# Placing a pair's sums and one cast of x later on VectorE, at the seam between a hand-planned schedule and a steady loop

## The chip, the cores and the metric

The kernel runs on one core of one Trainium2 chip. The metric is device time in microseconds; a profiled execution also has a span, from its first to its last instruction. Ratios are the mean time of one kernel's runs over the mean of the other kernel's runs of the same rounds, so not quite the ratio of the medians that are quoted beside them.

## The reference

```python
x: (16, 512, 1024) float32;  w1, w2: (1024, 768) float32
y1 = np.matmul(x, w1)
y2 = np.matmul(x, w2)
return np.tanh(y1) * y2
```

Every variant below gave correct outputs.

## The kernel before

The 8192 rows of x are 64 tiles of 128 rows. The first six are done plainly. The rest go in 29 pairs, and each pair makes two **units**, an even one for w1 (which ends in tanh) and an odd one for w2 (which ends in the multiply and the store). A unit uses a Strassen-type scheme: seven products p1 to p7 of 128 x 512 blocks of x with blocks of w, in place of eight. For that, a pair needs four sums of blocks of x on VectorE:

```python
def s_block(i, n, eng):
    s = spool.tile([P, KH, P], f16, tag=n, name=n)
    a, b, op = {"s1": ("a21", "a22", ALU.add), "s2": ("s1", "a11", ALU.subtract),
                "s3": ("a11", "a21", ALU.subtract), "s4": ("a12", "s2", ALU.subtract)}[n]
    pin((nc.vector if eng == "dve" else nc.gpsimd).tensor_tensor(s, st[i, a], st[i, b], op))
    st[i, n] = s

PRODUCTS = {"p1": ("a11", "b11"), "p2": ("a12", "b21"), "p3": ("s4", "b22"), "p4": ("a22", "t4"),
            "p5": ("s1", "t1"), "p6": ("s2", "t2"), "p7": ("s3", "t3")}
```

The blocks a11 to a22 come out of a DMA transpose of x in fp16, and VectorE makes the fp16 copy (the cast). After the products, VectorE adds two parts out of PSUM; one of the additions, c22, reads the bank that p4 then goes on accumulating into:

```python
# name: (engine, cost, due in slots, needs, ...)   [cut: the other operations of a unit]
"p2": ("pe", 0.65, -2, ["seed"], unit_product, (u, "p2", "a", False, True)),
"p3": ("pe", 0.65, 2, ["s5"], unit_product, (u, "p3", "d", False, True)),
"c12": ("dve", 0.55, 3, ["p3", "u2"], add_out, (u, "d", "u2", "c12")),
"p7": ("pe", 0.65, 3, ["u2"], unit_product, (u, "p7", "b", False, False)),
"c22": ("dve", 0.55, 4, ["p7", "s5"], add_out, (u, "b", "s5", "c22")),
"p4": ("pe", 0.65, 6, ["c22"], unit_product, (u, "p4", "b", False, True)),
```

Up to unit 9 the order on each engine is written out by hand (the planned part). From unit 10 on, each operation gets a time in slots of 0.65 us, the time from one product's start to the next in the trace (93.09 to 93.74 in the prediction's timeline), and the sorted times are the program order on every engine. Unit u begins at slot 7u. In the trace VectorE kept to that order where data were ready sooner: c22, ready at about 94.60 us (the prediction's estimate), ran at 96.09, behind s2. This is the code that the change touches:

```python
for i in range(FIRST, PAIRS):          # FIRST = 6
    z = 14 * i - 6
    at(slot(z - 7), blocks, i)
    for j, n in enumerate(("s1", "s2", "s3", "s4")):
        at(slot(z - 5.5 + 1.3 * j), s_block, i, n, "dve")
    at(slot(z - 1.4), out_scales, i)
    if i == FIRST:
        continue
    for h in range(2):
        if i > FIRST + 1:
            at(slot(z - 46 + 4 * h), load_x, HEAD + 2 * i + h)
        at(slot(z - 30 + 4 * h), abs_x, i, h)
    late = 1.1 * (i == FIRST + 1)
    at(slot(z - 25 + late), scale_x, i)
    for h in range(2):
        at(slot(z - 24 + late + 4 * h), cast_x, i, h, "dve")
        at(slot(z - 24 + late + 4 * h), transpose_x, i, h)
```

## Time and profile before

| | before |
|---|---|
| time, median of the first 3 runs | 317.22 us (316.65 to 317.24) |
| span of the profiled execution | 315.3 us |
| TensorE busy | 307.9 us (98%) |
| VectorE busy | 244.8 us (78%) |
| ScalarE busy | 230.5 us (73%) |

With TensorE busy for 307.9 of 315.3 us, a change of order on VectorE can help only where TensorE waits. The prediction shows the lines that say where. In timeline lines the columns are start, duration, engine, line, operation, output and inputs, shape and count; a bracket at the end tells how long the engine had been idle and what ended it.

### The profile page before, as it was taken

To read this page: it belongs to the slowest core of one execution; us is meant where nothing else is said; L and a number is where in the kernel's file an instruction comes from. 1 tells how busy PE (TensorE), PEld (TensorE's weight loads), DVE (VectorE), ACT (ScalarE), POOL (GpSimd) and SP (SyncE) were. 2 spreads that over 40 slices of the span, in tenths; PEclk is the share of its full clock that TensorE was granted. 3 is DMA by queue.
4 is the path that set the end of the run, shared out by engine and by line. 5 is a ranking of instruction groups with operands and counts; after the bars stand their busy time and mean duration, and the time that the engine had idled before them with its cause. 6 is when DMAs were issued, how large, how long until landed. Compare 5 with 4: busy or idle time off the path is not lost.

```text
span 315.3 us, 5481 instructions
## 1 busy us (share of the span) xinstructions
PE 307.9 (98%) x1890; PEld 185.5 (59%) x1895; DVE 244.8 (78%) x571; ACT 230.5 (73%) x453; POOL 4.3 (1%) x10
## 2 busy tenths in 40 slices
PE   8999999999998999999999999999999999999994
PEld 5756656666555555555555556555555555555652
DVE  2688978888887778877777897777789777777743
ACT  3788789786887777778777777877777778876551
POOL 0000000000000000000000000000000000000003
PEclk9999999999999999999999999999999999999998
DMA  7999498999999998999999989999998899996222
GB/s 289 406 400 369 95 311 245 262 263 264 308 318 267 287 278 258 246 231 287 268 255 242 285 239 224 299 252 283 242 251 265 263 246 282 234 238 168 101 101 102
DMA packets 82300, 80.59 MB, mean 256 GB/s; under 512 B 63584, under 2 KB 64096, under 8 KB 82272
## 3 DMA queue, kind: packets, MB, share of 16 engines
q1 hardware_dynamic: 81408, 78.27, 89.0%
q10 hardware_dynamic: 864, 1.97, 1.6%
q8 instruction: 15, 0.25, 0.3%
q14 instruction: 13, 0.11, 0.1%
HBM read 39.85 MB, written 25.17 MB: 206 GB/s over the span
## 4 chain that ended last, share of the span: by engine, by line
PE 86%; DMA 6%; DVE 3%; ACT 2%; issue 1%; DVEq 0%; SPq 0%; ACTq 0%
PE bank L401 79%; PE bank L267 4%; DMA x_f<-in_x_dram 3%; DMA xT<-x_h 3%; PE bank L270 2%; PE bank L223 1%; ACT junk L340 1%; DVE x_h L360 1%; DVE o L287 1%; DVE t L318 1%; ACT b L313 0%; DVE c L423 0%; DVE o L437 0%; ACT x_h L362 0%; DVE t L322 0%
## 5 line engine op out<-in xcount | busy, mean ns | idle before, releaser
L401 PE MATMUL bank<-t,s 128*128 128x384 f16 x696 | 131.6, 326 | 0.4 <-DVE t L318 0.4
L401 PEld LDWEIGHTS <-s 128*128 128x128 f16 x928 | 90.6, 98 | 61.1 <-issue 0.8
L401 PEld LDWEIGHTS <-xT 128*128 128x128 f16 x696 | 67.9, 98 | 48.0 <-issue 2.2
L401 PE MATMUL bank<-b,xT 128*128 128x384 f16 x464 | 93.8, 326 | 0.2 <-ACT b L313 0.2
L423 DVE TENSOR_TENSOR c<-bank,u 128x384 f32<-128x384 f32 x58 | 32.0, 554 | 43.6 <-PE bank L401 41.1
L340 ACT ACTIVATE junk<-x_f 128x1024 bf16<-128x1024 f32 x58 | 60.8, 1049 | 2.6 <-DMA x_f<-in_x_dram 2.5
L431 ACT ACTIVATE th<-c,out_r 128x384 f32<-128x384 f32 x58 | 35.3, 609 | 21.9 <-DVE c L423 21.9
L401 PE MATMUL bank<-t,xT 128*128 128x384 f16 x232 | 47.0, 326 | 0.8 <-DVE c L423 0.8
L401 PE MATMUL bank<-b,s 128*128 128x384 f16 x232 | 47.1, 327 | 0.0
L418 ACT ACTIVATE u<-bank 128x384 f32<-128x384 f32 x58 | 28.2, 487 | 19.7 <-PE bank L401 19.3
L360 DVE TENSOR_SCALAR x_h<-x_f,pr 128x1024 f16<-128x1024 f32 x55 | 41.0, 747 | 0.2
L414 ACT ACTIVATE bank<-bank 128x384 f32<-128x384 f32 x58 | 27.8, 481 | 12.7 <-DVE o L437 10.1
L423 DVE TENSOR_TENSOR c<-bank,s 128x384 f32<-128x384 f32 x58 | 32.2, 555 | 6.0 <-PE bank L401 5.0
L431 ACT ACTIVATE th<-bank,out_r 128x384 f32<-128x384 f32 x58 | 33.3, 573 | 4.5 <-PE bank L401 4.5
L437 DVE SCALAR_TENSOR_TENSOR o<-bank,out_r,th 128x384 f32<-128x384 f32 x58 | 35.4, 611 | 0.9 <-PE bank L401 0.9
L437 DVE SCALAR_TENSOR_TENSOR o<-c,out_r,th 128x384 f32<-128x384 f32 (+1 forms) x57 | 34.3, 606 | 0.4 <-ACT th L431 0.2
L418 ACT ACTIVATE s<-bank 128x384 f32<-128x384 f32 x58 | 27.8, 482 | 7.3 <-PE bank L401 5.0
L382 DVE TENSOR_TENSOR s<-xT 128x512 f16<-128x512 f16 x58 | 24.1, 417 | 0.1
L267 PE MATMUL bank<-wb,xTb 128*128 128x512 bf16 x91 | 23.9, 380 | 0.2
L270 PE MATMUL bank<-wb,xTb 128*128 128x256 bf16 x96 | 14.6, 273 | 0.0
L260 ACT ACTIVATE junk<-wf 128x768 bf16<-128x768 f32 (+1 forms) x13 | 12.8, 988 | 1.4 <-DMA wf<-in_w_dram 1.2
L267 PEld LDWEIGHTS <-xTb 128*128 128x128 bf16 x96 | 9.3, 99 | 7.5 <-DVE xTb L231 0.3
(49 smaller groups left out, 144.3 us busy)
## 6 DMA issues: line engine op xcount, KB each, us to landing
x_f<-in_x_dram SPq DMA_DIRECT2D x64, 512.0 KB, 6.0
out_dram<-o SPq DMA_DIRECT2D x62, 384.0 KB, 3.7
wf<-in_w_dram SPq DMA_DIRECT2D x12, 384.0 KB, 8.2
wf<-in_w_dram ACTq DMA_DIRECT2D x4, 384.0 KB, 7.8
xT<-x_h SPq DMA_TRANSPOSE x58, 3.9
out_dram<-o ACTq DMA_DIRECT2D x2, 192.0 KB, 2.1
out_dram<-o SPq DMA_DIRECT2D x2, 192.0 KB, 2.4
```

The costliest lines, as they stand in the source:

```text
L260: pin(nc.scalar.activation(junk[:, :n * N].rearrange("p (k n) -> p k n", n=N), w_f[t][:, k:k + n, :], ACT.Abs, accum_out=asum_w[t][:, j:j ...
L267: pin(nc.tensor.matmul(bank, hx[mt][:, k, :], w_b[t][k][:, :F], start=k == 0, stop=k == KO - 1))
L270: pin(nc.tensor.matmul(bank[:, at_:at_ + G], hx[mt][:, k, :], w_b[t][k][:, F:], start=k == 0 and mt % 2 == 0, stop=k == KO - 1, skip_group ...
L340: pin(nc.scalar.activation(junk[:, :K], xs[HEAD + 2 * i + h], ACT.Abs, scale=2.0 ** -12, accum_out=pair_sum[i][:, h:h + 1]))
L360: pin(nc.vector.tensor_scalar(xh, xs.pop(mt), pair_r[i][:, h:h + 1], None, ALU.mult))
L382: pin((nc.vector if eng == "dve" else nc.gpsimd).tensor_tensor(s, st[i, a], st[i, b], op))
L401: pin(nc.tensor.matmul(bank[:, cols], st[i, a][:, k, :], wt[t][b][:, k, cols], start=start and k == 0, stop=stop and k == KH - 1, skip_gro ...
L414: pin(nc.scalar.activation(ub[u]["b"][:, :Q], ub[u]["a"][:, :Q], ACT.Copy))
L418: pin(nc.scalar.activation(c, ub[u][bank][:, :Q], ACT.Copy))
L423: pin(nc.vector.tensor_tensor(c, ub[u][bank][:, :Q], ub[u][other], ALU.add))
L431: pin(nc.scalar.activation(th, v, ACT.Tanh, scale=rs[i][:, 0, h:h + 1]))
L437: pin(nc.vector.scalar_tensor_tensor(o[:, h, q * Q + cols.start:q * Q + cols.stop], v, rs[i][:, 1, h:h + 1], tanhs[i, h, q][:, cols], ALU. ...
```

## The change

Intent: at the seam between the planned part and the loop, let c22 of unit 10 run before things that are needed only later.

```diff
     for j, n in enumerate(("s1", "s2", "s3", "s4")):
-        at(slot(z - 5.5 + 1.3 * j), s_block, i, n, "dve")
+        at(slot(z - 5.5 + 1.6 * (i == FIRST) + 1.3 * j), s_block, i, n, "dve")
[cut]
     for h in range(2):
-        at(slot(z - 24 + late + 4 * h), cast_x, i, h, "dve")
-        at(slot(z - 24 + late + 4 * h), transpose_x, i, h)
+        at(slot(z - 24 + (1 + h) * late + 4 * h), cast_x, i, h, "dve")
+        at(slot(z - 24 + (1 + h) * late + 4 * h), transpose_x, i, h)
```

The first part moves the four sums of pair 6 by 1.6 slots. The second moves the second cast of pair 7, and the transpose that follows it, by 1.1 slots. No instruction is added or removed.

## The prediction

> **What bounds the kernel now.** I read the busy times first, then TensorE's waits, then the chain that ended last, then the timelines of TensorE and VectorE around the one wait that lies inside the long run of products.
>
> ```profile
> PE 307.9 (98%) x1890; PEld 185.5 (59%) x1895; DVE 244.8 (78%) x571; ACT 230.5 (73%) x453; POOL 4.3 (1%) x10
> ```
>
> TensorE is busy for 307.9 of 315.3 us, so an edit on VectorE can only pay where TensorE stands still for VectorE. In the waits of TensorE alone, the start-up lines apart, one matters:
>
> ```profile
> PE bank L401 <- DVE c L423: 0.8, 1, 0.8
> ```
>
> It happened once. The chain puts it in time:
>
> ```profile
> 87.97 6.29 DMA xT<-x_h
> ...
> 96.70 212.80 PE bank L401 x1300
> ```
>
> From 96.70 us to 309.50 us the chain is TensorE alone. Before that it passes through a DMA transpose that lands at 94.27 us and through VectorE. TensorE's timeline there (start, duration, engine, line, operation, count, idle before):
>
> ```profile
> 93.09 0.81 PE L401 MATMUL bank<-b,s 128*128 128x384 f16 x4
> 93.74 1.46 PE L401 MATMUL bank<-t,s 128*128 128x384 f16 x8
> 95.04 0.81 PE L401 MATMUL bank<-b,xT 128*128 128x384 f16 x4
> 96.70 0.81 PE L401 MATMUL bank<-t,xT 128*128 128x384 f16 x4 [0.84 <-DVE c L423]
> ```
>
> A product is four matmuls. Its printed length is 0.81 us, but one starts every 0.65 us (93.09, 93.74, two in the next line, 95.04). So the product at 96.70 was due at 95.04 + 0.65 = 95.69 us, and the real loss is 96.70 - 95.69 = **1.01 us**, of which the profile calls 0.84 idle. By the program's slots these are p3 of unit 10 (93.09), p7 of unit 10 and p5 of unit 11 (93.74), p2 of unit 11 (95.04) and p4 of unit 10 (96.70). p4 accumulates into a bank that VectorE's c22 must have read first. VectorE in those microseconds:
>
> ```profile
> 93.53 0.61 DVE L437 SCALAR_TENSOR_TENSOR o<-bank,out_r,th 128x384 f32<-128x384 f32 x1
> 94.29 0.43 DVE L382 TENSOR_TENSOR s<-xT 128x512 f16<-128x512 f16 x1
> 94.63 0.55 DVE L423 TENSOR_TENSOR c<-bank,u 128x384 f32<-128x384 f32 x1
> 95.10 0.75 DVE L360 TENSOR_SCALAR x_h<-x_f,pr 128x1024 f16<-128x1024 f32 x1
> 95.75 0.42 DVE L382 TENSOR_TENSOR s<-s,xT 128x512 f16<-128x512 f16 x1
> 96.09 0.55 DVE L423 TENSOR_TENSOR c<-bank,s 128x384 f32<-128x384 f32 x1
> ```
>
> c22 is the last line. It ends at 96.64 us and p4 starts 0.06 us later. Ahead of it stand three things nobody needs yet: s1 of pair 6, the second cast of pair 7, and s2 of pair 6.
>
> [...] 0.81 us printed against a pitch of 0.65, which is why I count 1.01 and not 0.84. [...] c22 had its product by about 94.60 us (worked out below) and still ran behind s2 at 96.09. [...] the x load issued at 87.38 us landed after 5.7 us, at 93.1, and the transpose issued behind it at 87.97 landed next, at 94.27. I use that in the second rival.
>
> **The change part by part.** No instruction is added or removed. The instruction orders show VectorE with 573 rows in both, TensorE, ScalarE and GpSimd in the same order (only buffer names differ), and one swap on the DMA queue. Everything lies in the one stretch around 94 to 98 us.
>
> Old order on VectorE: s1, c12, cast, s2, c22, s3, f00, s4, out scales. New order: c12, c22, s1, cast, s2, f00, out scales, s3, s4.
>
> Starts on VectorE follow each other faster than the durations say: 0.53 us after an o (96.89 to 97.42), 0.47 after a c, 0.34 after an s, 0.65 after a cast. The new times:
> - The o at 93.53 lets c12 start at 93.53 + 0.53 = 94.06. Its product p3 started at 93.09; elsewhere c12 follows its p3 by 0.92 (98.64 to 99.56), so it is ready at 94.01. It starts at 94.06, not 94.63.
> - c22 needs p7, which started at 93.74. Unit 11 shows c22 0.86 after its p7 (99.29 to 100.15), so 94.60 at the earliest; VectorE is free at 94.53. It ends near 94.60 + 0.55 = 95.15, add 0.06 to be seen: 95.21. p4 is due at 95.69. **Spare: 0.48 us.** The wait vanishes whole.
> - What moved back has room. s1 starts near 95.1, the cast at 95.4, s2 at 96.1, f00 at 96.7 (the stores that must have left its buffer land at 95.7 and 96.7), s3 and s4 by 97.7. With p4 at 95.69 and 0.65 per slot, p5 of unit 12 (needs s1) is due five slots on at 98.94, p6 (s2) at 100.89, p3 (s4) at 102.19, p7 (s3) at 102.84. At least 3 us to spare each. VectorE's next work, c12 of unit 11, cannot start before its p3 at 97.64 + 0.92 = 98.56, so the moved work fits into the 1.66 us that VectorE was idle there anyway.
>
> Sum: TensorE runs 1.01 us earlier from p4 of unit 10 on, and the chain after it is TensorE alone for 212.80 us, so it should all reach the end: 317.22 - 1.01 = **316.21 us**, a gain of 0.32%. VectorE's busy time stays at 244.8 us.
>
> **What the change can't touch.** In the steady part the same wait comes back, too short to be listed:
>
> ```profile
> 196.62 0.81 PE L401 MATMUL bank<-b,xT 128*128 128x384 f16 x4
> 197.32 0.81 PE L401 MATMUL bank<-t,xT 128*128 128x384 f16 x4
> ```
>
> The second was due at 197.27; c22 there ends at 197.26. p4 recurs every 9.09 us right after the stall (96.70, 105.79), and every 9.15 to 9.16 us later (188.16, 197.32, 206.47): 0.06 us per pair over some 21 pairs, about 1.3 us, my estimate. The edit's term applies to the first pair alone, so this stays.
>
> **Rivals.**
> 1. *A new wait takes the place of the old one.* The cast of pair 7 ends near 96.15 instead of 95.85, and c12 of unit 12 now stands 1.01 us earlier. Its VectorE queue has s1 of pair 7 just ahead, and that needs the transpose of this cast. In steady state c22 ends only 0.07 us before its p4 (105.72 against 105.79), so any delay of s1 would pass to TensorE in full. For it: the stretch is full (DMA share above 1 from 84 us on), and on the DMA queue a store (384 KB) and an x load (512 KB) now go ahead of the transpose. Against it: s1 of pair 7 would start at 104.03 - 1.01 = 103.02. The transpose was issued at 95.91 and landed 5.3 us later, at 101.2. Now it is issued at about 96.25; the two transfers ahead hold 0.9 MB, at some 400 GB/s 2.2 us more at worst, but the queue had gaps after 99 us (2 GB/s between 99 and 100). I put its landing at 101.0 to 103.0. If it does slip by 0.5 us past the need, half of the gain goes: 316.7.
> 2. *The gain is given back downstream*, because some other chain (x loads, ScalarE's sums, stores) holds the later part. Against it: no wait of TensorE after 96.70 is listed at all, and the period after the stall is shorter than the steady one, so nothing external sets it. Steady c22 hangs on TensorE's own earlier products through VectorE, so that loop moves as a whole. For it: I see only one execution. Full loss gives 317.2.
> 3. *Only noise moves.* The three runs lie within 0.59 us (316.65 to 317.24), more than half of the gain. The median may well hide it.
>
> **Range and chances.** Centre 316.2: rival 1 in part or run spread pulls towards 317, and nothing I see pulls far below 315.9. The range 315.6 to 317.2 holds all three. Two per cent is 6.3 us; no step here is worth more than 1.1 us, so faster by over 2% and slower by over 2% get 0.01 each and same 0.98.
>
> **What would show it.** Right: the span falls to about 314.3; the 0.84 us wait on c is gone from TensorE's waits; p4 of unit 10 starts 0.65 us after p2 of unit 11 (about 95.7); VectorE shows two c's in a row at about 94.1 and 94.6, then s, cast, s; the chain of TensorE work starts near 46 us and is unbroken to about 308.5. Wrong: a wait of TensorE on c about 9.1 us after p4, or an idle stretch of VectorE before s1 of pair 7 ended by a transpose (rival 1), or a steady period longer than 9.16 us (rival 2). The prediction would also fail if the planned part before 93 us shifts, which the unchanged orders speak against.

The "some 400 GB/s" of its first rival is what the trace of the kernel before shows: 393 to 450 GB/s in the busiest 1 us windows between 84 and 103 us.

## The result, and the profile after

| | before | after |
|---|---|---|
| median, 6 runs each | 317.22 us (316.65 to 317.68) | 316.59 us (316.10 to 317.09) |
| ratio | | 0.998 (95%: 0.9965 to 0.9996) |
| span, profiled execution | 315.3 us | 314.2 us |
| VectorE busy | 244.8 us | 244.4 us |

It is the same within 2%, and a small gain that is clear of noise. All outputs are right. Of TensorE's waits in the changed kernel, these are all that concern the products; the wait on c is gone:

```profile
PE bank L401 <- DVE t L318: 0.4, 1, 0.4
PE bank L401 <- ACT b L313: 0.2, 1, 0.2
```

The chain that ended last (start, duration, what) is now one piece of TensorE work from 46 us to 308.43 us:

```profile
46.01 262.42 PE bank L401 x1604
```

TensorE's timeline at the place of the old stall: p7 of unit 10 with p5 of unit 11, then p2 of unit 11, then p4 of unit 10:

```profile
93.66 1.46 PE L401 MATMUL bank<-t,s 128*128 128x384 f16 x8
94.96 0.81 PE L401 MATMUL bank<-b,xT 128*128 128x384 f16 x4
95.61 0.81 PE L401 MATMUL bank<-t,xT 128*128 128x384 f16 x4
```

p4 starts 0.65 us after p2, where it took 1.66 before. VectorE's timeline there:

```profile
93.45 0.61 DVE L437 SCALAR_TENSOR_TENSOR o<-bank,out_r,th 128x384 f32<-128x384 f32 x1
93.98 0.54 DVE L423 TENSOR_TENSOR c<-bank,u 128x384 f32<-128x384 f32 x1
94.51 0.56 DVE L423 TENSOR_TENSOR c<-bank,s 128x384 f32<-128x384 f32 x1
94.98 0.41 DVE L382 TENSOR_TENSOR s<-xT 128x512 f16<-128x512 f16 x1
95.32 0.74 DVE L360 TENSOR_SCALAR x_h<-x_f,pr 128x1024 f16<-128x1024 f32 x1
95.98 0.42 DVE L382 TENSOR_TENSOR s<-s,xT 128x512 f16<-128x512 f16 x1
```

c12 and c22 now run back to back; c22 ends at 95.07 us, 0.54 us before p4 is due.

So the profiled execution shows the whole predicted gain: its span is 1.1 us shorter. The median shows only 317.22 - 316.59 = 0.63 us. In this group the missing 0.4 us is not clear of noise: the interval of the ratio is a gain of 0.13 to 1.11 us, and 1.01 lies in it. Two later groups gave 0.92 and 0.62 us. Many of the experiments go into this part.

### The profile page after: what moved, and what is told of

Read it like the earlier page. It is cut to its first block, busy times and chain, and to the rows that moved or that the text cites. A ratio compares the mean times of both kernels' runs of the same rounds, so it can differ in the third digit from the quotient of the medians.

```text
span 314.2 us, 5487 instructions
## 1 busy us (share of the span) xinstructions
PE 308.0 (98%) x1895; PEld 185.4 (59%) x1895; DVE 244.4 (78%) x571; ACT 230.4 (73%) x453; POOL 4.3 (1%) x10
## 4 chain that ended last, share of the span: by engine, by line
PE 91%; DMA 3%; DVE 3%; ACT 1%; issue 0%; DVEq 0%; SPq 0%; ACTq 0%
PE bank L401 84%; PE bank L267 4%; DMA x_f<-in_x_dram 3%; PE bank L270 2%; PE bank L223 1%; DVE o L287 1%; DVE t L318 1%; ACT b L313 0%; DVE x_h L360 0%; ACT junk L340 0%; DVE o L437 0%; ACT x_h L362 0%; DVE t L322 0%; PE bank L153 0%; DVE xTb L244 0%
## 5 line engine op out<-in xcount | busy, mean ns | idle before, releaser
L267 PE MATMUL bank<-wb,xTb 128*128 128x512 bf16 x96 | 25.0, 379 | 0.0
```

The source lines that it names most:

```text
L267: pin(nc.tensor.matmul(bank, hx[mt][:, k, :], w_b[t][k][:, :F], start=k == 0, stop=k == KO - 1))
```

## The experiments

All medians below are with the kernel before timed on the same chip in the same rounds. Executions start unevenly: TensorE's long stretch begins between 45.9 and 47.5 us, in the earliest and the latest profile 5.63 us after an x load landed (at 40.29 us in e_s_only, at 41.90 in e_cast_only). I therefore also give the **TensorE stretch**: from the start of that stretch in the chain of waits to its end in the last unit (before: 46.09 to 309.50, so 263.41 us; after: 262.42 us). It holds the stalls and leaves the start out, but it can be read only for the one profiled execution of each run. The **gap** below is the time from the start of p2 of unit 11 to the start of p4 of unit 10; without a stall it is 0.65 us. The **o** is the last multiply into an output tile ahead of this place on VectorE (at 93.53 us before).

| run | median, us | before in its rounds, us | ratio (95%) | TensorE stretch, us |
|---|---|---|---|---|
| group 1: e_s_only | 316.61 | 317.95 | 0.997 (0.995 to 0.999) | 262.57 |
| e_cast_only | 316.98 | 317.95 | 0.9984 (0.9963 to 1.0005) | 263.34 |
| e_more_ahead | 318.97 | 317.95 | 1.0041 (1.0018 to 1.0064) | 266.54 |
| e_after_again | 317.03 | 317.95 | 0.9981 (0.9964 to 0.9998) | 262.55 |
| group 2: e_before_again | 317.42 | 317.20 | 1.000 (0.9988 to 1.0013) | 263.41 |
| e_cast_later | 316.77 | 317.20 | 0.9981 (0.9968 to 0.9993) | 262.99 |
| e_load_behind | 315.99 | 317.20 | 0.996 (0.9947 to 0.9972) | 262.42 |
| e_all_pairs | 314.92 | 317.20 | 0.9921 (0.9908 to 0.9935) | 261.33 |
| group 3: e_after_third | 317.06 | 317.68 | 0.9974 (0.9957 to 0.9991) | 263.77 |
| e_load_behind_2 | 316.27 | 317.68 | 0.9951 (0.9938 to 0.9965) | 262.45 |
| e_all_pairs_2 | 315.24 | 317.68 | 0.9919 (0.9906 to 0.9932) | 261.33 |
| e_both | 314.91 | 317.68 | 0.9907 (0.9893 to 0.9921) | 261.33 |

**My theory** for the gain: the stall is the work that stands ahead of c22 on VectorE. **Rivals**: the transpose that s1 waits for sets p4's time whatever the order; or the sums and the cast each carry half.

### Half of the change: the sums alone (e_s_only)

```diff
+        at(slot(z - 5.5 + 1.6 * (i == FIRST) + 1.3 * j), s_block, i, n, "dve")
 (the lines of the cast as before)
```

> Half of the change alone: the four sums of pair 6 go 1.6 slots later, the cast of pair 7 stays. VectorE order: o, c12, cast, c22, s1, s2. My theory (work standing ahead of c22 on VectorE is the whole stall): c12 starts 0.53 us after the o, the cast 0.47 later, c22 0.65 after that and ends 0.55 later, so p4 of unit 10 starts 0.10 us past its due time instead of 1.01. The gap between the starts of p2 of unit 11 and p4 is 0.75 us (before 1.66, after 0.65), the span 0.9 us under before. Rival (the transpose that landed at 94.27 us sets p4, through s1, whatever stands in front of c22): the gap falls to 0.65 here as in the full change. Rival (the sums and the cast each take half): the gap is near 1.2.

In TensorE's timeline p2 starts at 94.86 us and p4 at 95.61: a gap of 0.75 us, to the hundredth what the sum of the starts gave. The TensorE stretch is 0.84 us under before. Both rivals miss (0.65 and 1.2 us). The transpose of pair 6 even landed at 95.2 us here, 0.9 us later than before, and p4 was 0.10 us late. The sums alone bring most of the gain, because with s1 the wait for the transpose also leaves the place ahead of c22; the halves are not equal.

This half also leaves the transpose of pair 7 early: it was issued at 95.15 us and landed at 100.9, and p4 of unit 12 was on time. In the medians it is 0.42 us under the full change of the same group (316.61 to 317.03). That is not clear of noise, since the runs overlap, but nothing here shows that the second half of the change paid.

### The other half: the cast alone (e_cast_only)

```diff
+            at(slot(z - 24 + (1 + h) * late + 4 * h), cast_x, i, h, "dve")
+            at(slot(z - 24 + (1 + h) * late + 4 * h), transpose_x, i, h)
 (the line of the sums as before)
```

> The other half alone: the second cast of pair 7 goes behind c22, the sums stay. VectorE order: o, s1, c12, s2, c22, cast. My theory: s1 still waits for the transpose to about 94.2 us, c12 0.34 us later, s2 0.47 after, c22 0.34 after and 0.55 long: p4 starts 0.36 us past its due time, a gap of 1.01 us between the starts of p2 and p4, and the span 0.65 us under before. Rival (the transpose sets p4): the gap stays near 1.66 us, no gain.

VectorE's and TensorE's timelines of this run:

```profile
94.97 0.61 DVE L437 SCALAR_TENSOR_TENSOR o<-bank,out_r,th 128x384 f32<-128x384 f32 x1
96.15 0.43 DVE L382 TENSOR_TENSOR s<-xT 128x512 f16<-128x512 f16 x1 [0.58 <-DMA xT<-x_h]
```
```profile
96.48 0.81 PE L401 MATMUL bank<-b,xT 128*128 128x384 f16 x4
97.90 0.81 PE L401 MATMUL bank<-t,xT 128*128 128x384 f16 x4 [0.60 <-DVE c L423]
```

The gap is 1.42 us and not the 1.01 expected. The order did what it should, but s1 started 1.18 us after the o and not 0.76: the transpose of pair 6 landed later in this execution. 1.01 + 0.42 = 1.43. So the stall has **two terms**, the work ahead of c22 and the lateness of a transpose. The ratio's interval includes 1. The span, expected 0.65 us under before, was 1.3 us over it: this execution began its stretch only at 47.53 us, and the stretch was 0.07 us shorter.

### More work ahead of c22 (e_more_ahead)

```diff
-        at(slot(z - 5.5 + 1.3 * j), s_block, i, n, "dve")
+        at(slot(z - 5.5 + (0.45 if i == FIRST else 1.3) * j), s_block, i, n, "dve")
```

> The suspected cost enlarged: from the kernel before, s3 and s4 of pair 6 are put ahead of c22 too. VectorE order: o, s1, s2, c12, cast, s3, s4, c22. My theory: two more sums of 0.34 us each ahead of c22, and s2 right behind s1 costs about 0.08 us more, so the gap between the starts of p2 and p4 grows from 1.66 to about 2.4 us and the span by 0.7 to 0.8 us over before; the time near 317.9 us. Rival (TensorE would have stood still in that place anyway, for the transpose): gap and span as before, 317.2 us.

TensorE's timeline, then busy time by stretch (stretch; its length; per engine busy us and instructions; granted TensorE clock; DMA share; GB/s):

```profile
95.07 0.81 PE L401 MATMUL bank<-b,xT 128*128 128x384 f16 x4
98.43 0.48 PE L401 MATMUL bank<-t,xT 128*128 128x384 f16 x1 [2.55 <-DVE c L423]
```
```profile
95.50:98.40 2.90, 0.38 (x3) 0.10 (x1) 2.87 (x8) 0.99 (x2) 0.00 (x0) 0.93 1.06 235
98.40:99.90 1.50, 1.47 (x5) 0.71 (x5) 0.57 (x2) 1.49 (x3) 0.00 (x0) 0.50 1.04 226
99.90:101.40 1.50, 1.50 (x6) 0.74 (x5) 0.00 (x0) 0.84 (x4) 0.00 (x0) 0.50 0.94 273
101.40:103.00 1.60, 1.60 (x12) 0.93 (x11) 0.26 (x1) 1.19 (x3) 0.00 (x0) 1.00 0.98 339
```

The gap is 3.36 us. I expected about 2.4. Here s1 started 1.67 us after the o (VectorE had waited 1.06 us for the transpose), 0.91 more than 0.76, and 2.4 + 0.91 = 3.31. And there is a third cost that I had not foreseen: the granted clock was 0.50 after a TensorE idle of 2.55 us, with 11 matmuls in the 3 us after it, and the products started at 98.43, 99.66, 100.94 and 101.82 us, the first three 1.23 and 1.28 us apart. The stretch before, 95.5 to 98.4 us, has a mean clock of 0.93; if that is 1.00 and then 0.50, the clock was down from about 98.0 us, before TensorE resumed (my estimate: 0.07 x 2.90 / 0.50 = 0.41 us). From 101.4 it is 1.00 again. After idles of 0.34 (e_cast_later), 0.77 (e_before_again), 0.84 (before) and 1.07 us (e_after_third) the next product came after 0.64 to 0.65 us. The TensorE stretch grew by 3.1 us: 3.36 - 1.66 = 1.70 from the gap and 1.45 from the slow clock (98.43 to 101.82 + 0.65 = 102.47, 4.04 us, for the four products that took 2.59 before, 96.70 to 99.29). The median rose by 1.02 us only, so this execution was a bad one; its time, 320.25 us, was the slowest of the six. The other five have mean clocks of 0.998 or 0.999 where this one has 0.992, so the slow clock is shown in one execution. Another took 320.15 us at 0.999; why is not shown.

### The kernel before once more (e_before_again)

No edit.

> The kernel before, unchanged, for a second profile of it. In two variants that keep s1 ahead of c12 the transpose of pair 6 landed later than in the first profile (VectorE stood 0.58 and 1.06 us for it). My theory: the stall of the kernel before is a fixed part of about 0.8 us (work ahead of c22) plus whatever that transpose is late, so here the gap between the starts of p2 of unit 11 and p4 of unit 10 is 1.66 us plus the time by which s1 starts later than 0.76 us after the o's start. Rival (the stall is a constant of the order alone): 1.66 us within 0.05 wherever s1 starts. Timed: same as before, ratio 1.000 within 0.002.

VectorE's and TensorE's timelines:

```profile
93.72 0.61 DVE L437 SCALAR_TENSOR_TENSOR o<-bank,out_r,th 128x384 f32<-128x384 f32 x1
94.40 0.43 DVE L382 TENSOR_TENSOR s<-xT 128x512 f16<-128x512 f16 x1
```
```profile
95.23 0.81 PE L401 MATMUL bank<-b,xT 128*128 128x384 f16 x4
96.81 0.81 PE L401 MATMUL bank<-t,xT 128*128 128x384 f16 x4 [0.77 <-DVE c L423]
```

s1 started 0.68 us after the o, 0.08 earlier than in the first profile, and the gap is 1.58 us, 0.08 smaller than 1.66. That is the two-term rule, to the hundredth. The constant-stall rival falls, here by little (it allowed 0.05 us), and more clearly in the two variants above, where the rule gave 1.43 and 3.31 us for the measured 1.42 and 3.36. This run is also the null of the timing: ratio 1.000.

### The changed kernel twice more (e_after_again, e_after_third)

No edit. For e_after_again I still held the missing 0.4 us for spread of the start, and a later stall for the rival. Its profile turned this round for e_after_third: the change made the *second* transpose of pair 7 later, and s1 of pair 7, which needs it, stands ahead of c12 and c22 of unit 12, so p4 of unit 12 is late by as much.

> The changed kernel once more, to see how far single executions spread: the profile of the first showed a span 1.07 us under before, the median of six runs only 0.63 us under. My theory: the stall of 1.01 us is gone in every execution (gap of p2 to p4 0.65 us), and the rest is spread in the loads of the first 46 us; median 316.2 to 316.9. Rival (in some executions a later stall replaces it): this profile shows a wait of TensorE on VectorE's c after 96 us, or a gap above 0.75 us between two products there.

> The changed kernel beside its three improved versions on one chip. Theory: the part of the predicted 1.01 us that the medians did not show (0.63 us in the first six runs) is lost in some executions before s1 of pair 7, which waits for a transpose that the change itself made later. So here: gap p2 to p4 of unit 10 0.65 us; p4 of unit 12 late by 0 to 0.5 us; median 0.4 to 1.0 us under before. Rival (the missing part is spread of the start alone): no wait before s1 of pair 7, and the version with the load behind is no faster.

In all three profiles of the changed kernel p4 of unit 10 is on time (gap 0.65 us). At p4 of unit 12 they differ. In the first, the transpose was issued at 96.1 us and landed 6.8 us later, at 102.9, and s1 started at 102.96 us, 0.05 after VectorE was free: no loss. In e_after_again it landed 6.9 us after 96.4, s1 came 0.17 us late and p4 0.11 us: a gap of 0.76 us there, just over the 0.75 set as the rival's sign. Its median, 317.03 us, also lies above the 316.2 to 316.9 expected, though before was at 317.95 on that chip. In e_after_third, VectorE and TensorE near 104 us:

```profile
102.58 0.74 DVE L360 TENSOR_SCALAR x_h<-x_f,pr 128x1024 f16<-128x1024 f32 x1
104.53 0.43 DVE L382 TENSOR_TENSOR s<-xT 128x512 f16<-128x512 f16 x1 [1.21 <-DMA xT<-x_h]
```
```profile
104.39 0.81 PE L401 MATMUL bank<-b,xT 128*128 128x384 f16 x4
106.28 0.81 PE L401 MATMUL bank<-t,xT 128*128 128x384 f16 x4 [1.07 <-DVE c L423]
```

From start to start that is 1.89 us, a loss of 1.24, more than the 0 to 0.5 expected: the same stall as the one removed, one pair later. That execution took 317.82 us, more than the median of the kernel before in the same rounds. Here even the transpose of pair 6 was late: s1 of pair 6 waited 0.41 us, which cost TensorE nothing, as c22 was already done, but put the cast and so the next transpose (issued at 97.0 us) back.

### Later still (e_cast_later)

```diff
-            at(slot(z - 24 + (1 + h) * late + 4 * h), cast_x, i, h, "dve")
+            at(slot(z - 24 + (1 + 4 * h) * late + 4 * h), cast_x, i, h, "dve")
 (and transpose_x the same)
```

> The changed kernel with the second cast of pair 7 put later still, behind s3. Its transpose is issued about 1.6 us later than in the changed kernel (96.1 us there, landing 6.8 us later, 0.05 us after VectorE was free for s1 of pair 7). Theory (that transpose is now the nearest limit: the first rival of the prediction): VectorE stands idle before s1 of pair 7, and p4 of unit 12 comes late by 0.3 to 1.5 us; span 0.3 to 1.5 us over the changed kernel. Rival (the slack is larger[...]): p4 of unit 12 on time within 0.1 us, span as the changed kernel.

VectorE's and TensorE's timelines:

```profile
103.53 0.42 DVE L382 TENSOR_TENSOR s<-xT 128x512 f16<-128x512 f16 x1 [0.47 <-DMA xT<-x_h]
```
```profile
105.27 0.81 PE L401 MATMUL bank<-t,xT 128*128 128x384 f16 x4 [0.34 <-DVE c L423]
```

The product before started at 104.12, so p4 followed it after 1.15 us and the loss is 0.50, in the range expected. The transpose, issued 1.5 us later than in the first profile of the changed kernel, landed 0.6 us later (97.6 + 5.9 = 103.5). So the slack is nil, as the theory has it, though the later issue cost less than its own delay; why is not shown.

### The x load behind the transpose (e_load_behind, e_load_behind_2)

The change also let two transfers go ahead of the transpose on the DMA queue. Before, it was issued at 95.9 us, behind one store; after, at 96.1, behind a second store (384 KB) and an x load of 512 KB for pair 9, which stands at slot 74 where the transpose stands at 74.2. This edit puts the load behind again and leaves the store:

```diff
-                at(slot(z - 46 + 4 * h), load_x, HEAD + 2 * i + h)
+                at(slot(z - 46 + 4 * h + 0.4 * (i == FIRST + 3 and h == 0)), load_x, HEAD + 2 * i + h)
```

> The changed kernel with one x load (512 KB, pair 9) put behind that transpose on the DMA queue instead of ahead of it. Theory: the transpose lands 1 to 1.5 us sooner, near 101.6 us instead of 102.9, VectorE does not wait before s1 of pair 7, and p4 of unit 12 is on time (0.65 us after the product before) in this profile; the time is 0.0 to 0.2 us under the changed kernel. Rival (the load was not in its way): lands at 102.9 as before and the small wait stays.

> The version with the x load behind the transpose, again, now beside the changed kernel. Theory: faster than the changed kernel by 0.1 to 0.5 us in the median, no wait before s1 of pair 7, 1.0 to 1.2 us under before. Rival: as the changed kernel within 0.1 us.

TensorE in e_load_behind_2 at p4 of unit 12:

```profile
104.11 0.81 PE L401 MATMUL bank<-b,xT 128*128 128x384 f16 x4
104.76 0.81 PE L401 MATMUL bank<-t,xT 128*128 128x384 f16 x4
```

On time, in both profiles. Beside the changed kernel on the same chip the median is 0.79 us lower (317.06 to 316.27), more than the 0.1 to 0.5 I had expected, and the six runs span 0.6 us (315.93 to 316.53) where those of the changed kernel span 1.55 (316.27 to 317.82). Against the kernel before, the medians now differ by 1.21 and 1.41 us, so the 1.01 us of the prediction is there in full, and 0.2 to 0.4 us more: the stretch is only 0.96 to 0.99 us shorter, and where the rest comes from is not shown. One part of the expectation missed: the transpose landed at 102.5 and 102.0 us in these two profiles, 0.4 to 0.9 us sooner than 102.9, not 1 to 1.5. What is gained is mainly that it no longer slips past its need. Its need is VectorE's readiness for s1 at 102.9 to 103.3 us.

### The sums later for every pair (e_all_pairs, e_all_pairs_2), and both together (e_both)

The edit is against the changed kernel; e_both has the edit of the load as well.

```diff
-        at(slot(z - 5.5 + 1.6 * (i == FIRST) + 1.3 * j), s_block, i, n, "dve")
+        at(slot(z - 5.5 + 1.6 + 1.3 * j), s_block, i, n, "dve")
```

> The changed kernel with the later place of the sums for every pair, not the first alone, so that c12 and c22 of every even unit run back to back. Theory: the 0.06 us that each steady pair loses at p4 comes from s1 and s2 standing ahead of c22; with them behind it the period of p4 falls from 9.155 to about 9.09 us, 21 times, so the span is about 1.0 to 1.3 us under the changed kernel, near 313.1 us, and the time some 2 us under before. Rival (the 0.06 us is set by ScalarE or the loop's own latency): the period stays at 9.15 us and the span near 314.3 us.

> The later sums for every pair, again, beside the changed kernel. Theory: 2.0 to 2.5 us under before, 1.3 to 1.9 us under the changed kernel; no gap between matmuls above 0.19 us from 95 to 300 us, although the transpose of pair 7 may land after 103 us, because s1 of pair 7 stands behind c22 here. Rival (the first result was that chip's): less than 1 us under the changed kernel.

> The later sums for every pair and the x load behind the transpose together. Theory: TensorE is already without a gap from 95 us to the last unit with the sums alone, so the load's place is worth nothing more: same as the version with the sums for every pair, within 0.2 us. Rival (the transposes still cost something): another 0.2 to 0.5 us.

VectorE near p4 of unit 12, and the chain, in e_all_pairs:

```profile
103.06 0.56 DVE L423 TENSOR_TENSOR c<-bank,u 128x384 f32<-128x384 f32 x1
103.64 0.56 DVE L423 TENSOR_TENSOR c<-bank,s 128x384 f32<-128x384 f32 x1
104.11 0.42 DVE L382 TENSOR_TENSOR s<-xT 128x512 f16<-128x512 f16 x1
```
```profile
46.04 261.33 PE bank L401 x1604
```

c12 and c22 come first in every pair. p4 of the even units recurs every 9.10 us (186.98 to 196.08 to 205.18 in e_all_pairs_2) where it took 9.15 to 9.16 before, and TensorE's 1604 instructions take 261.33 us in all three profiles, 1.09 us less than the same 1604 in the changed kernel's 262.42. In e_all_pairs the transpose of pair 7 landed 7.9 us after its issue at 96.2, at 104.1, later than in two of the three profiles of the changed kernel, and TensorE lost nothing: s1 behind c22 no longer blocks it. e_all_pairs_2 is 1.82 us under the changed kernel on the same chip and 2.44 under before, both as expected. e_both is the best of all, 314.91 us, 0.33 us under e_all_pairs_2 in the medians; but its TensorE stretch in the profile is the same 261.33, so this difference seems to lie outside the stretch. I expected 0.2 at most. The size is the rival's (0.2 to 0.5), but these profiles show no transpose that costs TensorE anything. What makes it, or whether it is only the start (45.96 against 46.38 us in the two profiles), stays open.

## Why the prediction was right or wrong

**Right: the time and its class.** 316.59 us against 316.2, in the range 315.6 to 317.2. In the medians of the three groups the gain is 0.62 to 0.92 us, and not the 1.01 of the sum.

**Right: the stall and its size.** The due time by the pitch (1.01 us lost, and not the 0.84 printed) holds: the TensorE stretch shrank from 263.41 to 262.42 us in the first profile of the changed kernel. The order of VectorE, the starts of c12 and c22 and the spare (0.54 us for a predicted 0.48) came out within 0.1 us. The trace prints a product longer, 0.81 us, than its pitch of 0.65. One term was seen and not drawn out: part of the stall is the transpose that s1 waits for, which varied: 0.68, 0.76, 1.18 and 1.67 us from the o to s1 in four executions that had s1 ahead of c12. So 1.01 is one execution's value; the second gave 0.93.

**Right, but sized too small: the first rival.** It named the mechanism, namely that the second transpose of pair 7 comes later and c22 of unit 12 has no slack. The transpose took 5.3 us to land before; in the changed order it took 6.8, 6.9 and 7.5 us, so 1.5, 1.6 and 2.2 more. The term "2.2 us more at worst" held in these three (e_all_pairs, another order, took 7.9). What failed is the discount from it, that "the queue had gaps after 99 us", and with it the landing "at 101.0 to 103.0". Without the discount the prediction's own numbers give 96.25 + 5.3 + 2.2 = 103.75. The landings were 102.9, 103.3 and 104.5 us, the last also issued 0.7 us later than the 96.25 assumed, against a need near 103. The losses at p4 of unit 12 were 0, 0.11 and 1.24 us, where the prediction reckoned with a slip of 0.5. That this held the median back is shown by e_load_behind_2 beside the changed kernel: with the load behind the transpose it is 0.79 us faster, and its profile has no slip. How often the unprofiled runs slipped can't be seen.

**Wrong: the second rival.** Nothing further down the loop gave the gain back; with the load behind, the stretch after p4 of unit 12 has no listed wait.

**Noise, the third rival,** is real: executions of one kernel spread by 0.35 to 2.2 us in a group, the start alone by 1.6 us over the profiles (45.92 to 47.53). The TensorE stretch takes the start out, in profiled executions.

**Right: what the change can't touch.** The estimate of 1.3 us for the steady part was 1.09 us when e_all_pairs took it away.

One slip of wording: the order on the DMA queue (the x load landed at 93.1 us, the transpose issued behind it at 94.27) that the prediction says it uses "in the second rival" is used in the first of its list.

**Open**: why a transpose's time to land varies so much at one place of one program (6.8, 6.9 and 7.5 us in three profiles of the changed kernel), what makes e_both's last 0.33 us, and the 0.2 to 0.4 us by which e_load_behind's gain exceeds the stall.

## What to carry to other kernels

When one engine is the bound and runs without a gap, find what it waited for even once, and order the engine that serves it by when the *bound* engine needs each result: what frees a bank comes first, what prepares the next pair after it (c22 ahead of the sums in every pair took 1.09 us off TensorE's stretch here), above all if that may itself wait for a DMA (s1 waited up to 1.21 us for its transpose in e_after_third, and p4 came 1.24 us late). Measure a stall by when the instruction was due, not by the idle time printed (1.01 against 0.84 us here). Moving work later moves its consumers' deadlines too: follow the moved cast to its transpose and to the next place where that is needed, and look at what slips ahead of it on the DMA queue (one x load put back behind the transpose: 0.79 us in the median).
